# Order of side work beside the tensor engine in a hybrid decoder trunk: sums tied behind newer vector work, loads, squares and scalings spaced differently

## The chip, the cores and the metric

One core of one Trainium2 chip. The metric is the device time of one launch in microseconds (us). The tensor engine is called PE, the vector engine DVE, the scalar engine ACT, GpSimd POOL, and the engine that issues most of the transfers SP. A time of before is the median of several launches; the profile is of one launch of its own.

## The reference

One layer of a decoder trunk over 2048 tokens of width 1024, in float32. All of it is computed from x, a conditioning vector c and the weights:

```python
mod = (c_act @ w_ada[l] + b_ada[l])[:, None, :]
sh1, sc1, g1, sh2, sc2, g2 = jnp.split(mod, 6, axis=-1)
h = rms_norm(x) * (1.0 + sc1) + sh1
x = x + g1 * token_mixer(h, ...)      # retention | HGRN2 | GLA
h = rms_norm(x) * (1.0 + sc2) + sh2
x = x + g2 * conv_ffn(h, ...)         # up, causal conv of width 3, silu gate, down
return rms_norm(x) * final_gain
```

The token mixer projects h once and splits the columns into four retention heads (a fixed decay per head), eight HGRN2 heads and four GLA heads (decays that depend on the data, per key channel). Each group runs a causal linear recurrence over the tokens, gets a norm per head and a swish gate, and one output projection follows.

## The kernel before

The tokens are cut into four blocks b = 0 to 3 of 512. The first part of the program, to about 1140 us, is the mixer: for each block it runs seven units in the order h0, g, h1, h2, h3, r0, r1 (an h unit is two HGRN2 heads, g the GLA heads, an r unit two retention heads), then the output projection in two halves. The rest is the feed-forward part, in two halves of 1024 tokens, with products over sums and differences of blocks (so fewer multiplications), for which sums of the weights and of the activations are made beforehand, during the mixer.

Each float32 product is three PE matmuls on values split into a high and a low part (`split3`, L290 to L292); the high part is a cast on ACT (L278, L342), the low part a subtraction on DVE.

A unit projects (names ps...), then runs its recurrence as a chain of steps (`gated`, `retention`). For an h unit these are: the diagonal dt, masked into `near` on DVE (L722); seven levels lv..._1 to lv..._64, each a PE matmul (L737), after which DVE scales q (L743) and k (L745) for the next level and masks the scores (L749; for wide levels ACT copies, L756, L760); the transposed keys kT (L770, copied by ACT at L773); the update u of the state; `carry`, four steps on DVE (L681) and copies of the state into a wide tile W on ACT (L683, and L674 for the first chunk); the output o (L149), a norm of it (`post`: L630 on ACT, L632, L633, `newton` at L180 to L185, L636, and the gate at L637 on DVE), and its transpose oT (L643). Names carry the unit, the block and the step: `lvh2_2_16` is level 16 of unit h2 in block 2. The gate itself is made in `tok_evac`: ACT copies the values (L613) and takes a sigmoid (L614), DVE multiplies (L615).

What sets the order: PE's instructions stand as the program writes them, and the program is written by a `Clock` that keeps a time of its own in us and calls a step when its due time has come (`clock.at(us, fn)`), a next step of a chain after a gap, or riders at the next level (`ride(fn, soon, late)`). The other engines' instructions, SP's transfers among them, are ordered by the framework's scheduler, by priority. Each engine then takes its instructions strictly in that order. For some side work the program ties the order: `marked(op)` remembers an instruction, and `pinned(fn)` issues what fn emits only after the remembered one. Before, the low-part subtractions (L282, L348, L450) and the k scaling of a level (L745) were marked.

The side work that matters here:

- `ada_next`: a row of the conditioning matrix w_ada is loaded (L264) and, pinned, reduced on DVE (L222).
- `weight_sums` and `early_sums`: two loads (L992, L993), four DVE additions of 128x512 in two steps (L998, L999 and L1002, L1003), two stores (L1005, L1006). `in_turn` runs the steps, pinned, LAND and LAND + 2 us after the loads were called; a second job of a unit comes LAND + 5 after the first.
- `norm1_stat(b + 1)`: the statistics of the next block's first norm. Eight rows x of 128x512 are loaded (L574) STAT_GAP = 2.4 us apart, each squared on ACT (L385, L388) and added on DVE (L389, tile san1); PE sums over partitions (ssn1).
- `out_finish(b)`: the second norm of a block. Its eight scalings t2 (L1077 on DVE, L1078 on ACT, a store at L1079) come NORM_GAP apart. The residual x1 is made at L1058.

Row tiles x, t2 and others share a ring of six buffers (`tmp`); a load into it waits, in SP's queue, until the buffer is free.

Of the kernel before, what the change touches and what calls it, by code (L numbers as in the profile page):

```python
# [14 lines left out]
ALU = mybir.AluOpType  # L15
PSUM = bass.MemoryType.PSUM

P = 128
# [30 lines left out]
M512, M256, MF, ML, MT, MO, MS = 0.227, 0.12, 0.224, 0.5, 0.44, 1.7, 0.85  # L49
LEVEL_GAP = (3.2, 4.2)  # L50
POST_GAP = 14.0
LAND = 6.0
FIRST_GAP = 1.8, 0.8
RIDE = (1.8, 6.0), (3.4, 7.6)
STAT_GAP, NORM_GAP = 2.4, 1.6


class Clock:
# [64 lines left out]
def trunk(ctx, tc, xT, vecs, cvec, cst, rope, msk, wada, win, walow, wgla, wout, wup, wdown, out):  # L123
# [13 lines left out]
    clock = Clock()  # L137
# [8 lines left out]
    def tiled(out, lhs, rhs, start=True, stop=True):  # L146

        for g in range(0, P, 32):
            T.matmul(out[g:g + 32], lhs[:, g:g + 32], rhs(g) if callable(rhs) else rhs, start=start, stop=stop)  # L149
# [12 lines left out]
    def small(name, n=8):  # L162
        return pc.tile([P, n], F32, tag="sm", name=name, bufs=8)

    V, S, G, T = nc.vector, nc.scalar, nc.gpsimd, nc.tensor
# [28 lines left out]
    r = small("lbr", 4)  # L194
# [40 lines left out]
    SH1, SC1, G1, SH2, SC2, G2 = (mod[:, i * 8:i * 8 + 8] for i in range(6))  # L235
# [13 lines left out]
    def marked(op):  # L249

        mark[:] = [op.ins]
# [109 lines left out]
    def rstd(acc, name, bc, then, bank=None, gap=4.5):  # L361

        bank = bank or late_ps

        def first():
            p = bank("ss" + name)
            for c in range(NCH):
                tiled(p[:, c:c + 1], acc[:, c * P:(c + 1) * P], ones)
            x, r = small("ms" + name, NCH), small("rs" + name, NCH)
            with tc.high_priority(offset=CHAIN):  # L370
                V.tensor_scalar(x[:], p[:, 0:NCH], 1.0 / D, EPS, op0=ALU.mult, op1=ALU.add)
                newton(x, r, NCH)
            clock.at(gap, lambda: second(r))

        def second(r):
            p = bank("bc" + name)
            for c in range(NCH):
                T.matmul(p[:, c * P:(c + 1) * P], r[:, c:c + 1].to_broadcast([P, P]), ident, start=True, stop=True)
            S.copy(bc, p[:])
            then()  # L380
        return first

    def sumsq(acc, x, k, name, sl=slice(0, TB), first=None, room=None):
        if k == 0 if first is None else first:
            S.activation(acc[:, sl], x[:, sl], AF.Square)  # L385
        else:
            sq = (room or late)(f"sq{name}{k}")
            S.activation(sq[:, sl], x[:, sl], AF.Square)  # L388
            V.tensor_tensor(acc[:, sl], acc[:, sl], sq[:, sl], op=ALU.add)  # L389
# [15 lines left out]
    bc1 = {}  # L405
    done = set()
# [162 lines left out]
    def norm1_stat(b):  # L569
        acc = new_acc(f"n1_{b}")  # L570

        def part(k):
            x = tmp(f"x{b}_{k}")
            nc.sync.dma_start(x[:], xT[b, :, k, :])  # L574
            sumsq(acc, x, k, f"n1_{b}_")
        for k in range(KD):
            clock.at(STAT_GAP * k, lambda k=k: part(k))
        bc1[b] = new_bc1(b)
        clock.ride(rstd(acc, f"n1_{b}", bc1[b][:], lambda: done.add(("n1", b)), gap=14.0), 24.0, 28.0)

    def norm1_h(b):
        clock.until(lambda: ("n1", b) in done)
# [25 lines left out]
    def tok_evac(vsg, pss):  # L608
        v, sg = vsg
        for j, ps in enumerate(pss):  # L610
            p3 = ps[:].rearrange("p (c n) -> p c n", n=256)
            c2 = slice(2 * j, 2 * j + 2)
            S.copy(v[:, c2, :], p3[:, :, 0:P])  # L613
            S.activation(sg[:, c2, :], p3[:, :, P:256], AF.Sigmoid)  # L614
            V.tensor_tensor(sg[:, c2, :], sg[:, c2, :], p3[:, :, P:256], op=ALU.mult)  # L615

    def tok_evac4(vsg, pss, at):

        v, sg = vsg
        for c, ps in enumerate(pss):  # L620
            gate = ps[:, at + P:at + 256]
            S.copy(v[:, c, :], ps[:, at:at + P])
            S.activation(sg[:, c, :], gate, AF.Sigmoid)
            V.tensor_tensor(sg[:, c, :], sg[:, c, :], gate, op=ALU.mult)

    def post(o, sg, name):

        o8 = o[:].rearrange("p c (h e) -> p (c h) e", e=64)
        sq = late("osq" + name)
        S.activation(sq[:], o[:].rearrange("p c e -> p (c e)"), AF.Square)  # L630
        ms = small("oms" + name)
        V.tensor_reduce(ms[:], sq[:].rearrange("p (a e) -> p a e", e=64), axis=mybir.AxisListType.X, op=ALU.add)  # L632
        V.tensor_scalar(ms[:], ms[:], 1.0 / 64, EPS, op0=ALU.mult, op1=ALU.add)  # L633
        rs = small("ors" + name)
        newton(ms, rs, 8)
        V.tensor_tensor(o8, o8, rs[:].unsqueeze(2).to_broadcast([P, 8, 64]), op=ALU.mult)  # L636
        V.tensor_tensor(o[:], o[:], sg[:], op=ALU.mult)  # L637

    def transposed(b, pos, o, name):

# [250 lines left out]
    def unit_r(b, r, pos):  # L891
        nm = f"r{b}_{r}"
        if r == 0:
            rots[b] = pu.tile([P, NCH, 2, 32], F32, tag="rope", name="rope" + nm, bufs=1)
            nc.sync.dma_start(rots[b][:], rope[b])
        cos, sin = (rots[b][:, :, i, :] for i in range(2))
        kk = pu.tile([P, NCH, P], F32, tag="kk", name="kk" + nm)
        kc = pu.tile([P, TB], F32, tag="k", name="kc" + nm, bufs=3)
        q = p1.tile([P, 2, TB], F32, tag="qbd", name="q" + nm, bufs=3)
        vsg = tok_tiles(nm)  # L900
        pss = tf512("qkvg" + nm, 22 + 4 * r)
        a, bb = ([tmp(f"{n}{i}{nm}") for i in range(2)] for n in ("ra", "rb"))
        for c, ps in enumerate(pss):
            S.copy(a[0][:, c * P:(c + 1) * P], ps[:, 0:P])
            S.copy(a[1][:, c * P:(c + 1) * P], ps[:, P:256])
        tok_evac4(vsg, pss, 256)
        s4 = sin.unsqueeze(2).to_broadcast([P, NCH, 2, 32])
        for x, y in zip(a, bb):
            x8 = x[:].rearrange("p (c g n) -> p c g n", c=NCH, n=32)
            x4 = x[:].rearrange("p (c g t n) -> p c g t n", c=NCH, t=2, n=32)  # L910
            y4 = y[:].rearrange("p (c g t n) -> p c g t n", c=NCH, t=2, n=32)
            V.tensor_tensor(y4[:, :, :, 0, :], x4[:, :, :, 1, :], s4, op=ALU.mult)
            V.tensor_tensor(y4[:, :, :, 1, :], x4[:, :, :, 0, :], s4, op=ALU.mult)
            V.tensor_tensor(x8, x8, cos.unsqueeze(2).to_broadcast([P, NCH, 4, 32]), op=ALU.mult)
            V.tensor_tensor(x4[:, :, :, 0, :], x4[:, :, :, 0, :], y4[:, :, :, 0, :], op=ALU.subtract)
            V.tensor_tensor(x4[:, :, :, 1, :], x4[:, :, :, 1, :], y4[:, :, :, 1, :], op=ALU.add)
        kd = c_all[:, C_KD + 2 * r:C_KD + 2 * r + 2]
        V.tensor_tensor(kk[:].rearrange("p c (h n) -> p c h n", n=64),
                        a[1][:].rearrange("p (c h n) -> p c h n", c=NCH, n=64),
                        kd.unsqueeze(1).unsqueeze(3).to_broadcast([P, NCH, 2, 64]), op=ALU.mult)  # L920
        clock.chain(retention(nm, b, r, pos, a[0], kk, kc, q, vsg), 14.5 if b < 2 else 11.0)

    def retention(nm, b, r, pos, a, kk, kc, q, vsg):
        v, sg = vsg
# [50 lines left out]
    x1 = [None] * KD  # L975
# [35 lines left out]
    def in_turn(*steps):  # L1011
# [6 lines left out]
        for i, _ in enumerate(steps):  # L1018
            clock.at(LAND + 2.0 * i, go)

    def all_done():
        while waiting:
            waiting.pop(0)()
# [21 lines left out]
    def out_half(b, half, acc=None, after_pieces=None, begun=(), own=None):  # L1045
        all_done()
        for i in range(4):
            wp, pss = begun[i] if i < len(begun) else (out_piece(b, half, i), None)
            if i == 3 and after_pieces:
                after_pieces()  # L1050
            for m in (2 * i, 2 * i + 1):
                if half == 0:
                    x1[m] = x_tile(f"x1_{b}_{m}", m)
                    nc.sync.dma_start(x1[m], xT[b, :, m, :])
                ps = pss[m % 2] if pss else acc_ps(f"y{b}_{half}_{m}")
                out_part(b, half, wp, ps, m, range(3, 4) if pss else range(4))
                with tc.high_priority(offset=HOT):
                    V.scalar_tensor_tensor(x1[m], ps[:], G1[:, m:m + 1], x1[m], op0=ALU.mult, op1=ALU.add)  # L1058
                if half == 1:
                    with tc.high_priority(offset=HOT):  # L1060
                        sumsq(acc, x1[m], m, f"n2_{b}_", room=own)
        held[0] -= 4
# [143 lines left out]
    for b in range(NB):  # L1206
        pos = 0
# [4 lines left out]
        for i, (kind, u) in enumerate(ORDER):  # L1212
# [4 lines left out]
            if b and i:  # L1217
# [5 lines left out]
                for n, fn in enumerate(job):  # L1223
                    clock.at((30.0 if i == 1 else 14.0 if (b, i) == (1, 4) else 0.1) + (LAND + 5.0) * n, fn)
            mk[kind](b, u, pos)
# [17 lines left out]
    with tc.high_priority(offset=300):  # L1243
        A = {}
        for i in range(2):
            r = tmp(f"r0{i}_0_0")
# [382 lines left out]
    for k in range(4):  # L1629
        x = t2k(f"hr0_3_{k}")  # L1630
# [117 lines left out]
```

## Time and profile before

| | us |
|---|---|
| median of 3 runs | 2422.54 |
| lowest, highest run | 2421.09, 2425.87 |
| profiled execution | 2418.1 |
| its span | 2416.3 |
| PE busy in the span | 2382.3 |
| DVE busy | 1811.7 |
| ACT busy | 1229.3 |
| PE idle, all of the span | 34.0 |

The profiled execution takes 1.8 us more than its span. PE's idle time is the span less its busy time; 16.0 us of it lie before 120 us, 5.9 between 120 and 1080, and 12.2 after. In a list of waits each row names who waited, for whom (the instruction that ended last by the profile, which need not be the one whose data was needed), how long in total, how often, and the longest. In a timeline each row has the start, the duration, the engine, the line, the operation, the tiles, and in brackets the idle time of the engine before it with its releaser; several instructions that follow each other are one row with a count.

### The profile page before, as it was taken

What the parts mean: (1) busy time and instruction counts of PE and PEld (TensorE: products, weight loads), DVE (VectorE), ACT (ScalarE), POOL (GpSimd) and SP (SyncE); (2) the same over time, 40 slices, a digit from 0 to 9 for tenths busy, and PEclk for the clock granted to TensorE, in tenths of its full rate; (3) what the DMA queues carried; (4) which work ended last, traced back from release to release, by engine and by line L of the source; (5) the groups of instructions that cost most, each with busy time, mean ns of one, the idle gap of its engine ahead of it and who ended that gap; (6) DMA issues with size and microseconds to landing.
All of it is one profiled execution on the core that took longest, in us unless ns stands there. A gap on an engine that the chain in (4) does not pass through costs nothing.

```text
span 2416.3 us, 51796 instructions
## 1 busy us (share of the span) xinstructions
PE 2382.3 (99%) x20523; PEld 1962.8 (81%) x20523; DVE 1811.7 (75%) x3391; ACT 1229.3 (51%) x2191; POOL 154.2 (6%) x275
## 2 busy tenths in 40 slices
PE   7999999999999999999999999999999999999998
PEld 5788878878788878888788888888878888888887
DVE  7687766877577746767988888966878787778666
ACT  4565445644565446535645554554545454555442
POOL 1000000000000000001000000000010110000000
PEclk9999999999999999999999999999999999999999
DMA  7665676896788758778554444686765444447663
GB/s 273 228 214 186 226 271 224 293 329 237 258 311 290 259 187 284 267 260 295 178 170 155 148 155 144 229 281 218 226 204 173 144 149 139 153 151 271 210 196 118
DMA packets 228883, 525.78 MB, mean 218 GB/s; under 512 B 25848, under 2 KB 28832, under 8 KB 228640
## 3 DMA queue, kind: packets, MB, share of 16 engines
q1 hardware_dynamic: 225440, 511.98, 63.1%
q0 software_dynamic: 3200, 10.49, 1.2%
q8 instruction: 161, 2.64, 0.4%
q14 instruction: 82, 0.67, 0.1%
HBM read 392.87 MB, written 129.50 MB: 216 GB/s over the span
## 4 chain that ended last, share of the span: by engine, by line
PE 84%; DVE 6%; DMA 5%; issue 3%; ACT 1%; SPq 0%; POOL 0%; DVEq 0%; ACTq 0%; POOLq 0%
PE X L290 6%; PE X L291 6%; PE X L292 6%; PE Z L291 3%; PE Z L292 3%; PE Z L290 3%; PE dX L290 3%; PE dX L292 3%; PE dX L291 3%; PE psqkvgr L290 3%; PE psqkvgr L291 2%; PE psqkvgr L292 2%; PE psvgh L290 2%; PE y L290 2%; PE y L291 2%
## 5 line engine op out<-in xcount | busy, mean ns | idle before, releaser
L290 PE MATMUL X<-B,A 128*128 128x512 f32 x572 | 223.1, 390 | 0.5 <-ACT u L1424 0.3
L291 PE MATMUL X<-B,A 128*128 128x512 f32 x572 | 222.8, 389 | 0.3 <-DVE B L1121 0.2
L292 PE MATMUL X<-B,A 128*128 128x512 f32 x572 | 222.6, 389 | 0.0
L1121 DVE TENSOR_TENSOR dA<-rd,dA 128x512 fp32r<-128x512 f32 x154 | 106.1, 690 | 89.8 <-ACT dA L1120 89.6
L1120 ACT CAST dA<-rd 128x512 fp32r<-128x512 f32 x154 | 95.6, 621 | 143.7 <-PE dX L292 58.0
L290 PE MATMUL dX<-dB,dA 128*128 128x512 f32 x396 | 154.1, 389 | 1.3 <-DVE y L1606 1.3
L292 PE MATMUL dX<-dB,dA 128*128 128x512 f32 x396 | 154.0, 389 | 0.0
L291 PE MATMUL dX<-dB,dA 128*128 128x512 f32 x396 | 154.0, 389 | 0.0
L1121 DVE TENSOR_TENSOR A<-s,A 128x512 fp32r<-128x512 f32 x176 | 120.6, 686 | 39.5 <-ACT A L1120 39.4
L290 PE MATMUL psvgh<-hvgh,ha 128*128 128x256 f32 x480 | 140.3, 292 | 0.0
L1120 ACT CAST A<-s 128x512 fp32r<-128x512 f32 x176 | 108.5, 617 | 56.9 <-PE Z L292 41.9
L291 PE MATMUL psvgh<-lvgh,ha 128*128 128x256 f32 x480 | 135.6, 283 | 0.0
L292 PE MATMUL psvgh<-hvgh,ha 128*128 128x256 f32 x480 | 135.6, 282 | 0.0
L290 PEld LDWEIGHTS X<-B,A 128*128 128x128 f32 x572 | 107.3, 188 | 24.0 <-ACT u L1424 1.1
L291 PEld LDWEIGHTS X<-B,A 128*128 128x128 f32 x572 | 107.4, 188 | 23.0 <-DVE B L1121 1.0
L292 PEld LDWEIGHTS X<-B,A 128*128 128x128 f32 x572 | 107.4, 188 | 22.3
L291 PE MATMUL Z<-B,A 128*128 128x512 f32 x308 | 120.5, 391 | 1.4 <-DVE B L1121 1.2
L290 PE MATMUL Z<-B,A 128*128 128x512 f32 x308 | 120.3, 391 | 0.1
L292 PE MATMUL Z<-B,A 128*128 128x512 f32 x308 | 119.9, 389 | 0.0
L1120 ACT CAST A<-r 128x512 fp32r<-128x512 f32 x132 | 82.3, 623 | 63.8 <-PE Z L292 58.5
L1121 DVE TENSOR_TENSOR A<-r,A 128x512 fp32r<-128x512 f32 x132 | 90.6, 687 | 31.8 <-ACT A L1120 31.6
L1121 DVE TENSOR_TENSOR dB<-rb,dB 128x512 fp32r<-128x512 f32 x154 | 105.6, 687 | 9.9 <-ACT dB L1120 9.5
(480 smaller groups left out, 6714.3 us busy)
## 6 DMA issues: line engine op xcount, KB each, us to landing
gs<-yv SPq DMA_DIRECT2D x154, 256.0 KB, 3.0
rb<-gs SPq DMA_DIRECT2D x154, 256.0 KB, 4.2
r<-wup SPq DMA_DIRECT2D x143, 256.0 KB, 3.5
s<-sumsu SPq DMA_DIRECT2D x132, 256.0 KB, 3.0
wada<-wada SPq DMA_DIRECT2D x48, 512.0 KB, 4.9
rd<-sumsd SPq DMA_DIRECT2D x88, 256.0 KB, 3.9
rd<-wdown SPq DMA_DIRECT2D x66, 256.0 KB, 3.8
x<-xT SPq DMA_DIRECT2D x64, 256.0 KB, 5.9
```

The costliest lines, as they stand in the source:

```text
L290: T.matmul(ps, lhs[0], rhs[0], start=first, stop=False, skip_group_check=more)
L291: T.matmul(ps, lhs[0], rhs[1], start=False, stop=False, skip_group_check=more)
L292: T.matmul(ps, lhs[1], rhs[0], start=False, stop=last, skip_group_check=more)
L1120: S.copy(hi, src)
L1121: V.tensor_tensor(lo, src, hi, op=ALU.subtract)
```

## The change

Five edits; no instruction is added or taken away on any engine, only places in the queues change.

```diff
-LAND = 6.0
+LAND = 7.5
-STAT_GAP, NORM_GAP = 2.4, 1.6
+STAT_GAP, STAT_LAND, NORM_GAP = 2.4, 3.0, 2.0
...
         def part(k):
             x = tmp(f"x{b}_{k}")
             nc.sync.dma_start(x[:], xT[b, :, k, :])
-            sumsq(acc, x, k, f"n1_{b}_")
+            clock.at(STAT_LAND, lambda: sumsq(acc, x, k, f"n1_{b}_"))
...
-        clock.ride(rstd(acc, ...), 24.0, 28.0)
+        clock.ride(rstd(acc, ...), 26.0, 30.0)
...
-            V.tensor_tensor(sg[:, c2, :], sg[:, c2, :], p3[:, :, P:256], op=ALU.mult)
+            marked(V.tensor_tensor(sg[:, c2, :], sg[:, c2, :], p3[:, :, P:256], op=ALU.mult))
...
-            V.tensor_tensor(sg[:, c, :], sg[:, c, :], gate, op=ALU.mult)
+            marked(V.tensor_tensor(sg[:, c, :], sg[:, c, :], gate, op=ALU.mult))
...
-        V.tensor_tensor(o[:], o[:], sg[:], op=ALU.mult)
+        marked(V.tensor_tensor(o[:], o[:], sg[:], op=ALU.mult))
...
-        clock.chain(retention(nm, b, r, pos, a[0], kk, kc, q, vsg), 14.5 if b < 2 else 11.0)
+        clock.chain(retention(nm, b, r, pos, a[0], kk, kc, q, vsg), 14.5 if b < 3 else 11.0)
...
-                    V.scalar_tensor_tensor(x1[m], ps[:], G1[:, m:m + 1], x1[m], op0=ALU.mult, op1=ALU.add)
+                    marked(V.scalar_tensor_tensor(x1[m], ps[:], G1[:, m:m + 1], x1[m], op0=ALU.mult, op1=ALU.add))
```

The gate products (L615, L624), the last product of `post` (L637) and the residual (L1058) are now marked, so pinned work stands behind them. Sums fall due 1.5 us later after their loads, a second job 12.5 instead of 11 us after the first. A row's square is called 3.0 us after its load. t2 scalings are 2.0 instead of 1.6 apart. The retention of block 2 starts 3.5 us later by the program's clock, as that of blocks 0 and 1 does already. On PE only that last edit is seen: the matmuls of r2_0 and r2_1 stand some 3.5 us later among the others; elsewhere PE's list is the same.

DVE, unit h2 of block 1, the carry of the state (L681, tiles Sc and S2) before the output oh1_2; wsd1 is a weight sum. Before:

```order
L749 COPY_PREDICATED nearh1_3_0_6758<-m_all_87,lvh1_3_2_6876 128x64x2
L681 SCALAR_TENSOR_TENSOR Sc_6918<-S2_107,eh1_2_5628,uh1_2_6901 128x64
L998 TENSOR_TENSOR wsd1_2_6813<-wsd1_1_6812 128x512
L681 SCALAR_TENSOR_TENSOR Sc_6918<-Sc_6918,eh1_2_5628,uh1_2_6901 128x64
L999 TENSOR_TENSOR wsd1_2_6813<-wsd1_2_6813,wsd1_0_6811 128x512
L681 SCALAR_TENSOR_TENSOR Sc_6918<-Sc_6918,eh1_2_5628,uh1_2_6901 128x64
L1002 TENSOR_TENSOR wsd1_0_6811<-wsd1_0_6811,wsd1_1_6812 128x512
L681 SCALAR_TENSOR_TENSOR S2_107<-Sc_6918,eh1_2_5628,uh1_2_6901 128x64
```

And now, at the same place:

```order
L749 COPY_PREDICATED nearh1_3_0_6758<-m_all_87,lvh1_3_2_6881 128x64x2
L681 SCALAR_TENSOR_TENSOR Sc_6918<-S2_107,eh1_2_5628,uh1_2_6901 128x64
L681 SCALAR_TENSOR_TENSOR Sc_6918<-Sc_6918,eh1_2_5628,uh1_2_6901 128x64 x2
L681 SCALAR_TENSOR_TENSOR S2_107<-Sc_6918,eh1_2_5628,uh1_2_6901 128x64
L998 TENSOR_TENSOR wsd1_2_6813<-wsd1_1_6812 128x512
```

The four carry steps stand together, and the sum begins behind them.

ACT, unit h1 of block 1, before the output oh1_1_0, which reads W0; x2_4 is a row of block 2's first norm. Before:

```order
L817 ACTIVATE kh1_3_6134<-snh1_3_6342,oml_89 128x512
L1078 ACTIVATE t2_0_6_6358<-t2_0_6_6358,mod_102 128x512
L683 COPY W0_112<-Sc_6332 64x3x64 x2
L1078 ACTIVATE t2_0_7_6374<-t2_0_7_6374,mod_102 128x512
L674 COPY W0_112<-S5_110 64x64 x2
L388 ACTIVATE sqn1_2_4_6364<-x2_4_6362 128x512
```

And now:

```order
L817 ACTIVATE kh1_3_6134<-snh1_3_6334,oml_89 128x512
L278 CAST hvgh1_3_1_6625<-rvgh1_3_1_6627 128x1024
L388 ACTIVATE sqn1_2_4_6398<-x2_4_6349 128x512
L683 COPY W0_112<-Sc_6324 64x3x64 x2
L1078 ACTIVATE t2_0_5_6355<-t2_0_5_6355,mod_102 128x512
L1078 ACTIVATE t2_0_6_6372<-t2_0_6_6372,mod_102 128x512
```

A cast and the square of x2_4, which both need a load, now stand ahead of the copies into W0, and the scaled rows t2 behind them.

DVE, unit h2 of block 2, between the levels 8 and 32 (san1_3 is the sum of squares for block 3, omsh2_1_0 and orsh2_1_0 the norm of unit h1's output). Before:

```order
L697 TENSOR_TENSOR eh2_3_10092<-eh2_3_10092 128x4
L389 TENSOR_TENSOR san1_3_10088<-san1_3_10088,sqn1_3_5_10319 128x512
L389 TENSOR_TENSOR san1_3_10088<-san1_3_10088,sqn1_3_6_10394 128x512
L632 TENSOR_REDUCE omsh2_1_0_10400<-osqh2_1_0_10398 128x8
L743 TENSOR_TENSOR qbh2_2_9821<-qbh2_2_9821,eh2_2_9567 128x64x8
L633 TENSOR_SCALAR omsh2_1_0_10400<-omsh2_1_0_10400 128x8
L745 TENSOR_TENSOR kh2_2_9565<-kh2_2_9565,eh2_2_9567 128x32x8
```

And now, from the second half of the norm on:

```order
L745 TENSOR_TENSOR kh2_2_9565<-kh2_2_9565,eh2_2_9567 128x32x8
...
L389 TENSOR_TENSOR san1_3_10088<-san1_3_10088,sqn1_3_6_10465 128x512
L636 TENSOR_TENSOR oh2_1_0_10339<-oh2_1_0_10339,orsh2_1_0_10397 128x512
L826 TENSOR_TENSOR sqh2_3_10425<-sqh2_3_10425,fh2_3_10091 128x512
L637 TENSOR_TENSOR oh2_1_0_10339<-oh2_1_0_10339,sgh2_1_9316 128x512
L743 TENSOR_TENSOR qbh2_2_9821<-qbh2_2_9821,eh2_2_9567 128x32x16
L745 TENSOR_TENSOR kh2_2_9565<-kh2_2_9565,eh2_2_9567 128x16x16
L749 COPY_PREDICATED nearh2_2_0_10125<-m_all_87,lvh2_2_16_10523 128x8x16
L389 TENSOR_TENSOR san1_3_10088<-san1_3_10088,sqn1_3_7_10500 128x512
```

The addition of x3_6 has moved from ahead of L743 and L745 of level 8 to behind them, and the end of the norm now stands ahead of those of level 16.

More of the change, by code (lines that the diff above doesn't have):

```diff
@@ L578, in norm1_stat @@
         bc1[b] = new_bc1(b)
-        clock.ride(rstd(acc, f"n1_{b}", bc1[b][:], lambda: done.add(("n1", b)), gap=14.0), 24.0, 28.0)
+        clock.ride(rstd(acc, f"n1_{b}", bc1[b][:], lambda: done.add(("n1", b)), gap=14.0), 26.0, 30.0)
     def norm1_h(b):
```

## The prediction

> **What bounds the kernel now.** I read the page first: the engines' busy time, then the windows of the tensor engine (PE), to see how much idle time the touched stretch holds at all.
>
> ```profile
> PE 2382.3 (99%) x20523; PEld 1962.8 (81%) x20523; DVE 1811.7 (75%) x3391; ACT 1229.3 (51%) x2191; POOL 154.2 (6%) x275
> 120.00:1080.00 960.00, 954.11 (x13240) 1.00 0.74 256
> 360.00:480.00 120.00, 118.59 (x1944) 1.00 0.75 257
> 720.00:840.00 120.00, 117.79 (x1659) 1.00 0.80 277
> ```
>
> PE is the bound, 99% busy at a granted clock of 1.00. The order lists first differ near 150 us and agree again near 1130 us; the counts of instructions don't change. In 120 to 1080 us PE is idle for 960.00 - 954.11 = 5.9 us. No edit takes PE work away, so **5.9 us (0.24%) is the most this change can take out of that execution**, while what it can add has no such lid. Next the waits of PE, to see whose fault that idle time is.
>
> ```profile
> PE lvh L737 <- DVE orsh L180: 1.5, 1, 1.5
> PE kTh L770 <- DVE nearh L722: 1.0, 1, 1.0
> PE psqkvgr L291 <- issue: 1.0, 1, 1.0
> PE oh L149 <- DVE S L681: 0.4, 1, 0.4
> PE lvh L737 <- DVE nw L184: 0.4, 1, 0.4
> PE kTh L770 <- DVE kh L745: 0.3, 1, 0.3
> PE oh L149 <- ACT W L683: 0.3, 1, 0.3
> PE oTh L643 <- DVE oh L637: 0.3, 1, 0.3
> ```
>
> Columns: waiter, releaser, total us, times, longest. These eight make 5.2 of the 5.9 us. "issue" is nobody's data. The names of the vector engine (DVE) behind the arrow are only the instructions that happened to end last; what held them stands in the timeline.
>
> **Place 1, 480 us: a weight sum in front of a carry.**
>
> ```profile
> 478.46 0.69 DVE L998 TENSOR_TENSOR wsd<-wsd 128x512 f32<-128x512 f32 x1 [1.75 <-DMA wsd<-wdown]
> 479.86 0.28 DVE L681 SCALAR_TENSOR_TENSOR Sc<-Sc,eh,uh 128x64 f32<-128x64 f32 x1
> 481.07 0.38 PE L149 MATMUL oh<-W,qbh 128*32 128x128 f32 x5 [0.44 <-DVE S L681]
> wsd<-wdown SPq DMA_DIRECT2D x22, 512.0 KB, 5.6
> wsu<-wup SPq DMA_DIRECT2D x22, 512.0 KB, 5.9
> ```
>
> DVE stood 1.75 us for a load that had not landed, three of the four carry steps L681 queued behind it, ACT's copies L683 behind those, PE's oh1_2_0 behind these. In the new order all four carry steps stand ahead of L998 (marks), and the sum comes due 7.5 instead of 6.0 us after its load, against median landings of 5.6 and 5.9. The 0.44 goes: **-0.4**. The DVE work is only moved; what follows the sum then is lvh1_3_4's masks, which in this execution cause no wait.
>
> **Place 2, 439 us: gate products, and what the earlier row does in ACT's queue.**
>
> ```profile
> 436.92 0.35 ACT L613 COPY vh<-psvgh 128x256 f32<-128x256 f32 x1
> 437.58 0.42 DVE L615 TENSOR_TENSOR sgh<-sgh,psvgh 128x256 f32<-128x256 f32 x1 [0.65 <-ACT sgh L614]
> 438.86 0.43 DVE L722 COPY_PREDICATED nearh<-m_all,dth 128x256 f32<-128x256 uint32 x1
> 439.35 0.66 PE L770 MATMUL kTh<-c_all,kh 128*128 128x128 f32 x4 [0.99 <-DVE nearh L722]
> 447.48 0.70 ACT L683 COPY W<-Sc 64x192 f32<-64x192 f32 x2
> 447.92 0.45 PE L149 MATMUL oh<-W,qbh 128*32 128x128 f32 x8
> ```
>
> DVE waited 0.65 us for ACT's sigmoid, and ACT came late because scaled rows t2 (L1078) and a square stood ahead of L613. With t2 rows 2.0 apart and the square 3.0 behind its load, ACT has two of these fewer ahead of it; by my count of the new order the chain L613, L614, L615, L743, L745, L722 ends about 1.0 us earlier, and the 0.99 goes: **-1.0**.
>
> The same shift plants a new wait. In the new ACT queue the cast L278 and the square of x2_4 stand ahead of the two L683 copies; before, both came elsewhere. PE would now want W at 447.92 - 0.99 = 446.93. How long such rows take to land:
>
> ```profile
> x<-xT SPq DMA_DIRECT2D x64, 256.0 KB, 5.9
> 437.41 0.43 SPq L574 DMA_DIRECT2D x<-xT  x1
> 441.34 0.63 ACT L388 ACTIVATE sqn<-x 128x512 f32<-128x512 f32 x1 [0.24 <-DMA x<-xT]
> 420.09 0.43 SPq L574 DMA_DIRECT2D x<-xT  x1
> 428.46 0.63 ACT L385 ACTIVATE san<-x 128x512 f32<-128x512 f32 x1 [0.47 <-DMA x<-xT]
> ```
>
> From issue to the square that waited for it: 441.34 - 437.41 = 3.9 us for x2_3, 428.46 - 420.09 = 8.4 for x2_0; the median is 5.9. In the new SP queue x2_4 stands behind rqkvgr1_0_0, and I place its issue at 442.1 (an estimate). Landing after 3.9, 5.9 or 8.4 us, plus a square (0.63) and the copies (0.70), W is ready at 447.3, 449.3 or 451.8: a wait of 0.4, 2.4 or 4.9. I take a landing of 4.8, between the two nearest rows (3.9, and the median): **+1.3**, ends 0.4 and 4.9.
>
> [...]
>
> **Place 3, 458 us.**
>
> ```profile
> 457.59 0.42 DVE L745 TENSOR_TENSOR kh<-kh,eh 128x256 f32<-128x256 f32 x1
> 458.16 0.46 PE L737 MATMUL lvh<-qbh,kh 128*32 128x32 f32 x32 [0.37 <-DVE nw L184]
> ```
>
> lvh1_2_16 waited 0.4 for L745, behind L389 and L632 which ACT delivered late. The new order has the norm's chain and L821 ahead, ACT's osq square no longer sits behind three squares, and L745 should end about a us earlier: **-0.4**.
>
> **Place 4, 735 us: the largest wait.**
>
> ```profile
> 731.30 0.63 ACT L388 ACTIVATE sqn<-x 128x512 f32<-128x512 f32 x1 [2.81 <-DMA x<-xT]
> 731.97 0.69 DVE L389 TENSOR_TENSOR san<-san,sqn 128x512 f32<-128x512 f32 x1 [1.72 <-ACT sqn L388]
> 733.44 0.69 DVE L389 TENSOR_TENSOR san<-san,sqn 128x512 f32<-128x512 f32 x1 [0.78 <-ACT sqn L388]
> 734.65 0.68 DVE L743 TENSOR_TENSOR qbh<-qbh,eh 128x512 f32<-128x512 f32 x1
> 735.32 0.42 DVE L745 TENSOR_TENSOR kh<-kh,eh 128x256 f32<-128x256 f32 x1
> 735.88 0.46 PE L737 MATMUL lvh<-qbh,kh 128*32 128x32 f32 x32 [1.49 <-DVE orsh L180]
> 740.05 0.43 PE L737 MATMUL lvh<-qbh,kh 128*32 128x64 f32 x16
> 740.30 0.27 PE L149 MATMUL ssn<-c_all,san 128*32 128x1 f32 x14
> 724.01 2.36 SPq L574 DMA_DIRECT2D x<-xT  x3
> ```
>
> The squares asked for rows that had not landed; ACT stood 2.81 us, DVE 1.72 + 0.78, and L743/L745 for lvh2_2_16 stood behind. In the new order x3_2 to x3_5 are issued ahead of weight loads and sum stores in SP's queue, and x3_6's addition stands behind L745. DVE's 2.5 us of standing cover the 1.49 with 1.0 to spare: **-1.5**. Paid back next: lvh2_2_32 and the sum ssn1_3 would be wanted at 738.56 and 738.81. Ahead of them on DVE now stand the addition of x3_6, then L636, L826, L637 and L743/L745. x3_6 goes out behind the store L1006 of sumsu11, which waits for L1003, now behind lvh2_2_4's masks: about 727.9 (an estimate; x3_5 to x3_7 went out from 724.01 on in the last row above). With 5.9 us it lands at 733.8; square 0.63, addition 0.69, four steps of 0.69 and one of 0.42: 738.3, and with L749 and x3_7's addition (0.29 + 0.69) ssn1_3 is ready at 739.3, a wait of 0.5. With 8.4 us it is 3.0. I take **+0.7**, since each step also costs a hand-over. Then oTh2_1_0's 0.3 goes, its L637 standing four places earlier: **-0.3**.
>
> **The rest at nothing.** Of the eight waits, kTh L770 0.3 (same DVE order there), oh W 0.3 (178 us, ACT's own copies) and "issue" stay. The retention of b = 2 starts 3.5 us later in PE's own list: PE fills in with projection matmuls that stood there anyway, and the consumer of its last tile, y2_1, stands some 85 rows behind it; no wait between 840 and 1080 us gives it anything to win. t2's scalings (eight, L1077) only spread over 14.0 instead of 11.2 us; their stores are read in b = 3 at the earliest. If the retention's chain loses its cover, the nearest row is a hand-over like the 0.4 of oh.
>
> **Sum.** -0.4 - 1.0 + 1.3 - 0.4 - 1.5 + 0.7 - 0.3 = -1.6 us. The profiled execution took 2418.1 (span 2416.3 and 1.8 around it) and would take 2416.5. The median of the runs shown, 2422.54, lies 4.4 above it, so other executions wait more than this one shows, most likely for landings; I carry the difference over: 2422.54 - 1.6 = **2420.9**. A measurement of this kernel can tell about 0.2%, 4.8 us, from no change.
>
> **Rivals.** *Everything goes, nothing comes back.* The waits that the change reaches make 0.4 + 1.0 + 0.4 + 1.5 + 0.3 = 3.6 here. If the 4.4 us by which other runs are longer are landing waits of the same two kinds (sums and squares asked for too early), and half of them go too, it is -5.8: 2416.7. For it: median landings (5.6 to 5.9) sit right at the old 6.0. Against: PE shows only 3.6, and ACT's new order puts squares ahead of copies. Chance 0.24, all of it faster.
>
> *Slower: squares block ACT.* The rows are loaded earlier but their squares also stand earlier in ACT's queue, ahead of the W copies and the casts. It decides once rows land later than some 6 us. At 8.4: +4.9 instead of +1.3 at 447 us, +3.0 at 739 us, and x2_3's square ahead of kTh1_1's copy holds uh1_1 as well; if half of the 3.6 is lost in that queue, it is 4.9 + 3.0 - 1.8 = +6.1: 2428.6. For it: x2_0 did take 8.4. Against: the loads were moved ahead of other transfers. Chance 0.19, slower.
>
> *Nothing moves.* PE's list is nearly the same, and each wait freed is met by the next: 2422.5. Chance 0.09.
>
> **How the numbers follow.** The forecast has 0.48, with its own range of 2418.9 (gains of 3.6 and no new wait) to 2424.3 (new waits of 2.4 and 3.0), all within 0.2%. Same is 0.48 + 0.09 = 0.57, faster 0.24, slower 0.19. The range for 8 in 10 runs from 2416.0, just under the first rival, to 2428.0, just under the second.
>
> **What would show it.** Right: L998 of wsd1 behind all L681 with no DVE wait before the carry; no wait at lvh1_2_16, lvh2_2_16, oh1_2_0; the standing of ACT at L388 and of DVE at L389 near 731 us gone; small new waits at oh1_1_0 (releaser ACT L683) and ssn1_3 or lvh2_2_32. Wrong: PE's idle time in 120 to 1080 us above 5.9, or new waits after 780 us at the moved retention.

## The result and the profile after

| | median, us | lowest to highest | profiled execution's span |
|---|---|---|---|
| before | 2422.5 | 2419.9 to 2427.1 (9 runs) | 2416.3 |
| after | 2429.8 | 2425.8 to 2433.0 (9 runs) | 2424.2 |

The changed kernel is slower: ratio 1.0025, 95% interval 1.0016 to 1.0035, some 6 us; the medians lie 7.3 us apart and the two spans 7.9. The forecast was 2420.9 in a range of 2416.0 to 2428.0.

The profile after, first the busy line of the page and the windows of the tensor engine (columns: stretch, its length, PE busy, granted clock, DMA share, GB/s).

```profile
PE 2385.8 (98%) x20523; PEld 1964.8 (81%) x20523; DVE 1816.5 (75%) x3391; ACT 1232.6 (51%) x2191; POOL 153.8 (6%) x275
120.00:1080.00 960.00, 949.48 (x13170) 1.00 0.75 256
360.00:480.00 120.00, 116.99 (x1932) 1.00 0.76 260
600.00:720.00 120.00, 117.61 (x1643) 1.00 0.84 281
720.00:840.00 120.00, 117.29 (x1660) 0.99 0.81 283
```

PE's idle time between 120 and 1080 us has gone from 5.9 to 10.5 us, and over the whole span PE is also busy 3.5 us longer for the same matmuls (the half clock shown below makes 1.7 of that by my estimate; the rest isn't explained). The waits of PE in that stretch say where; its six largest new rows are these.

```profile
PE oh L149 <- issue: 2.7, 1, 2.7
PE kTh L770 <- DVE kh L745: 1.9, 1, 1.9
PE lvg L737 <- ACT atg L756: 1.4, 3, 0.7
PE oTg L643 <- DVE oTg L648: 1.2, 1, 1.2
PE lvh L737 <- issue: 0.9, 1, 0.9
PE oh L149 <- ACT W L683: 0.8, 1, 0.8
```

The waits that the change was to remove (lvh1_2_16, kTh1_1, oh1_2_0, lvh2_2_16, oTh2_1_0) are gone. These six came in their place, and only the last of them had a term in the forecast. Two kinds carry most of it.

**A reduction that waits for its row.** The timeline near kTh2_0 (607 us before, 610 now):

```profile
600.37 1.28 DVE L222 CUSTOM_DVE_ANT_0 wada<-wada,c_act,vec 128x1024 f32<-128x1024 f32 x1
601.69 0.33 SPq L264 DMA_DIRECT2D wada<-wada  x1
606.89 1.28 DVE L222 CUSTOM_DVE_ANT_0 wada<-wada,c_act,vec 128x1024 f32<-128x1024 f32 x1 [2.07 <-DMA wada<-wada]
609.96 0.41 DVE L745 TENSOR_TENSOR kh<-kh,eh 128x256 f32<-128x256 f32 x1
610.43 0.66 PE L770 MATMUL kTh<-c_all,kh 128*128 128x128 f32 x4 [1.93 <-DVE kh L745]
```

Rows of w_ada have one buffer. The load (L264) can go only when the reduction before it (L222) is over, at 601.69; the next reduction stands 2.07 us for it, and L745, for which PE waits, stands behind in the vector engine's queue. The vector engine's waits in the same stretch, of before and then of after:

```profile
DVE wada L222 <- DMA wada<-wada: 17.0, 10, 4.2
```
```profile
DVE wada L222 <- DMA wada<-wada: 24.4, 17, 3.2
```

Ten such stands have become seventeen.

**A stop for which no data is missing.** In the moved retention, the timeline of PE and three windows:

```profile
797.94 1.16 PE L950 MATMUL scr<-qr,kcr 64*32 64x128 f32 x64
799.03 0.42 PE L149 MATMUL oh<-W,qbh 128*32 128x128 f32 x8
...
800.60 0.29 PE L149 MATMUL oh<-vh,ath 128*32 128x64 f32 x7
803.60 0.33 PE L149 MATMUL oh<-vh,ath 128*32 128x64 f32 x9 [2.71 <-issue]
804.46 0.63 PE L292 MATMUL psqkvgr<-hqkvgr,ha 128*128 128x512 f32 x1
804.00:806.00 2.00, 2.00 (x6) 0.59 1.04 396
806.00:808.00 2.00, 2.00 (x6) 0.56 1.08 415
804.36:807.77 3.41, 3.41 (x9) 0.50 1.07 407
```

and of before, at the same matmuls:

```profile
793.03 1.16 PE L950 MATMUL scr<-qr,kcr 64*32 64x128 f32 x64
794.11 0.50 PE L290 MATMUL psqkvgr<-hqkvgr,ha 128*128 128x512 f32 x1
...
798.64 0.29 PE L149 MATMUL oh<-vh,ath 128*32 128x64 f32 x7
799.34 0.35 PE L149 MATMUL oh<-vh,ath 128*32 128x64 f32 x9 [0.41 <-issue]
```

PE stops in the middle of oh2_3_0, 2.71 us instead of 0.41, and then, from 804.36 on, runs at a granted clock of 0.50 for 3.4 us; half of that, 1.7 us, is my estimate of what it costs further. Before, twelve projection matmuls stood between scr2_0 and oh2_3_0; now the two follow each other directly.

### The profile page after: what moved, and what is told of

Read it like the earlier page. It is cut to its first block, busy times and chain, and to the rows that moved or that the text cites. A ratio compares the mean times of both kernels' runs of the same rounds, so it can differ in the third digit from the quotient of the medians.

```text
span 2424.2 us, 51792 instructions
## 1 busy us (share of the span) xinstructions
PE 2385.8 (98%) x20523; PEld 1964.8 (81%) x20523; DVE 1816.5 (75%) x3391; ACT 1232.6 (51%) x2191; POOL 153.8 (6%) x275
## 4 chain that ended last, share of the span: by engine, by line
PE 83%; DVE 6%; DMA 6%; issue 2%; ACT 2%; SPq 0%; DVEq 0%; POOL 0%; ACTq 0%; POOLq 0%
PE X L290 6%; PE X L292 6%; PE X L291 6%; PE Z L291 3%; PE Z L292 3%; PE Z L290 3%; PE dX L290 3%; PE dX L291 3%; PE dX L292 3%; PE psqkvgr L290 3%; PE psqkvgr L291 2%; PE psqkvgr L292 2%; PE y L290 2%; PE psvgh L290 2%; PE y L291 2%
```

## The experiments

Two theories came out of these readings: A, that PE ran out of instructions in the moved retention, and C, that reductions tied later keep the one row buffer; their rivals (B, D to G) stand with the runs. In the table L222 is the vector engine's total stand for rows of w_ada between 120 and 1080 us; "stop" is PE's wait near 800 us in oh2_3_0 with releaser issue, each in the one profiled execution.

| kernel | ratio to before, 95% interval | L222: us, times | stop, us |
|---|---|---|---|
| before | | 17.0, 10 | 0.41 |
| after | 1.0025, 1.0016 to 1.0035 | 24.4, 17 | 2.71 |
| marks_alone | 1.0030, 1.0018 to 1.0042 | 25.6, 16 | 1.51 |
| marks_rows_only | 1.0020, 1.0010 to 1.0031 | 29.4, 15 | 0.39 |
| rows_old_marks | 1.0007, 0.9999 to 1.0016 | 14.5, 10 | 2.13 |
| two_rows | 1.0007, 0.9998 to 1.0016 | 1.5, 2 | 2.33 |
| marks_two_rows | 0.9994, 0.9985 to 1.0003 | 2.0, 2 | 1.58 |
| two_rows_before | 0.9995, 0.9986 to 1.0003 | 2.5, 4 | 1.50 |
| ret_alone | 1.0011, 1.0002 to 1.0020 | 18.3, 10 | 2.67 |
| ret_undone | 1.0021, 1.0009 to 1.0033 | 26.9, 17 | 0.50 |
| ret_16_0 | 1.0002, 0.9993 to 1.0011 | 18.3, 10 | none |
| ret_12_5 | 1.0003, 0.9994 to 1.0012 | 18.8, 10 | none |
| stat_alone | 1.0002, 0.9993 to 1.0011 | 18.3, 11 | 1.31 |
| land_alone | 1.0004, 0.9995 to 1.0013 | 18.9, 10 | none |
| norm_alone | 1.0003, 0.9994 to 1.0012 | 17.0, 10 | 0.94 |
| land_norm | 1.0017, 1.0008 to 1.0026 | 17.7, 9 | none |
| best2 | 0.9996, 0.9987 to 1.0005 | 1.8, 2 | none |
| best3 | 0.9990, 0.9981 to 0.9999 | 1.3, 1 | 0.38 |
| best3_again | 1.0000, 0.9991 to 1.0009 | 1.9, 2 | 0.31 |
| best4 | 0.9994, 0.9985 to 1.0003 | 1.3, 1 | 0.25 |

### The marks

```diff
 marks_alone, from the kernel before: only the four new marked(...) at L615, L624, L637, L1058
```

> The kernel before with the four new marks alone (gate products L615 and L624, L637, L1058). Theory C: reductions of the rows of w_ada (L222) are tied later, the single buffer of those rows comes free later, the next row's load with it, and DVE then stands 1.5 to 2 us for it with level scalings L743 and L745 behind; that gives PE waits of about 2 us at kTh2_0 (607 us) and 1 us at lvg1_64 (401 us), against gains of 0.4 at oh1_2_0 and 1.0 at kTh1_1: +1 to +3 us in sum. By the prediction: -0.4 to -2, since the carry and L745 stand ahead of the sums.

1.0030: +7.1 us by itself, as much as the whole change and more than expected; the prediction's gain is refuted. At kTh2_0 PE waits 0.71 here, less than the 2 us expected. At lvg1_64 the wait is there as expected:

```profile
394.91 1.28 DVE L222 CUSTOM_DVE_ANT_0 wada<-wada,c_act,vec 128x1024 f32<-128x1024 f32 x1 [1.42 <-DMA wada<-wada]
397.56 0.69 DVE L826 TENSOR_TENSOR sqh<-sqh,fh 128x512 f32<-128x512 f32 x1
398.29 1.25 ACT L828 COPY qbh<-sqh 64x512 f32<-64x512 f32 x2 [5.96 <-DVE sqh L826]
406.04 0.67 PE L737 MATMUL lvg<-qbg,kg 64*32 64x128 f32 x30 [0.68 <-ACT atg L756]
```

The reduction's stand pushes L826 on the vector engine, for which ACT's queue stands 5.96 us (2.63 before), and the copies L756 behind it come late for lvg1_64. This wait of 0.9 to 1.0 us in all (two stops) stands in the profiles of the four kernels that tie the reductions behind the new marks and have one buffer, and in no other. Not every place tells the causes apart so well: at oh0_1_0 (179 us) PE waits 1.26 behind a stand of L222 here, but 1.49 in marks_two_rows and 1.99 in best2 (both below), where L222 doesn't stand there.

To tell the reductions from the sums, which are tied by the same marks, two lists of marks were kept:

```diff
-    def pinned(fn):
+    def pinned(fn, behind=mark):
-        with tc.issue_after(mark[0]):
+        with tc.issue_after(behind[0]):
 rows_old_marks, from the changed kernel: new marks enter only mark2
-                pinned(waiting.pop(0))
+                pinned(waiting.pop(0), mark2)
 marks_rows_only, from the kernel before with the new marks in mark2
-            pinned(lambda: ada(*loaded.pop()))
+            pinned(lambda: ada(*loaded.pop()), mark2)
```

> The changed kernel with the reductions of the rows of w_ada (L222) tied behind the old marks only; the sums stay behind the new ones, the other edits are kept. In the vector engine's waits between 120 and 1080 us, L222 stood for its row 17.0 us in 10 cases before, 24.4 in 17 in the changed kernel and 25.6 in 16 with the marks alone. Theory C (a reduction tied later frees the one buffer later, the next row is loaded later, the next reduction stands for it with carries and level scalings behind): L222 waits back at 16 to 19 us in 10 or 11 cases, and 3.5 to 6.5 us of the 7.3 go (ratio to before 1.0003 to 1.0016). Theory E (it is the sums behind the newer marks that crowd the vector engine): L222 aside, the time stays at 1.002 to 1.0035.

> The kernel before with the new marks for the reductions L222 alone; the sums stay tied to the old marks. Theory C: nearly all of the 7.1 us that the four marks cost by themselves, +4 to +7.5 us (ratio 1.0017 to 1.0031), L222 waits 24 to 27 us in 16 or 17 cases. Theory E: within 1.5 us of before.

Both times are as theory C has it: 1.0007 (the stands at 14.5 us in 10 cases, even under what was expected) and 1.0020 (29.4 in 15, more than the 24 to 27 expected). Theory E falls with them. Its direct opposite is to take the wait itself away and leave every tie where the change put it (the second pair of lines makes room for the second buffer):

```diff
 two_rows from the changed kernel, two_rows_before and marks_two_rows from the kernel before
-            raw = p1.tile([P, D], F32, tag="wada", name=f"wada{m}", bufs=1)
+            raw = p1.tile([P, D], F32, tag="wada", name=f"wada{m}", bufs=2)
-    mod = pc.tile([P, 48], F32, tag="mod", name="mod")
+    mod = vec[:, V_BADA:V_BADA + 48]
```

> The changed kernel with a second buffer for the rows of w_ada (mod moved into columns of another tile to make room), so that a row's load no longer waits for the reduction just before. Theory C: L222 waits under 6 us in all, the time 4 to 7 us under the changed kernel (ratio to before 0.9995 to 1.0013; the moved retention's 2 to 3 us stay). Theory E: 1.002 to 1.0035, as the changed kernel.

> The kernel before with the second buffer for the rows of w_ada. Theory C: L222's 17.0 us of standing fall under 6; the tensor engine waited little behind it there, so 0 to -3 us (ratio 0.9988 to 1.0000). Rival: rows of 512 KB issued earlier crowd the transfers of weights and of x, and the time rises by 1 to 3 us.

> The kernel before with the four new marks and the second buffer for the rows of w_ada, nothing else. Theory C: the marks' whole cost of 7.1 us was the rows' loads, so it stands where the second buffer alone does, 0.9985 to 1.0003, with L222 waits under 6 us. If the marks cost in another way too (sums and squares in new places): 1.0008 or more.

With a second buffer L222 stands 1.5 us in all, and the changed kernel comes down to 1.0007. With the marks alone and the second buffer the 7.1 us are gone altogether (0.9994, no different from the second buffer without the marks, 0.9995). So the marks' cost is the rows' one buffer, and nothing else that these runs can see. The kernel before had 17.0 us of such stands also; taking them away gave it nothing that can be measured (two_rows_before, 0.9995), and the rival's loss from crowded transfers didn't come either.

### The retention of block 2

```diff
 ret_alone, ret_16_0, ret_12_5 from the kernel before: 14.5, 16.0, 12.5 for b == 2
-  ... 14.5 if b < 2 else 11.0)
+  ... 14.5 if b < 3 else 11.0)
 ret_undone from the changed kernel: back to 14.5 if b < 2
```

> The kernel before with one edit alone: the retention of block 2 starts 3.5 us later (14.5 for b < 3). Theory A (PE ran out of instructions): in the changed kernel the 32 matmuls of scr2_0 and the 96 of oh2_3_0 stand directly together, PE stopped there for 2.7 us with the releaser issue, and the granted clock then fell to half for 3.4 us; that comes from the order alone, so this edit by itself gives +3 to +6 us over the kernel before, a wait with the releaser issue of over 2 us near 800 us at oh L149, and a stretch with a granted clock of 0.5 to 0.6 right behind it. Theory B (queues of the vector and scalar engines: squares and late sums): the retention's move is worth -1 to +1 us, and no clock dip is seen.

> The changed kernel with the retention of block 2 back at its old place (14.5 for b < 2), the other four edits kept. Theory A: some 4.5 of the 7.3 us go, so 2.5 to 3 us over the kernel before (ratio 1.001), no clock dip behind 800 us. Theory B: stays 6 to 8 us over the kernel before (ratio 1.0025 to 1.0035).

> The kernel before with the retention of block 2 at 16.0 instead of 11.0. On PE oh2_3_0 then stands directly ahead of scr2_0, so the two runs of small matmuls are still together, in the other order. Theory A (PE stops where such a run meets a late block of its instructions): a wait with releaser issue of over 2 us there, +2 to +4 us. Rival (the cost grows with how late the retention runs, through its chain): no such wait, +3 to +5 us from other waits at or, oTr or kTr.

> The kernel before with the retention of block 2 at 12.5 instead of 11.0: 12 projection matmuls still stand between scr2_0 and oh2_3_0, as before. Theory A: within 1.5 us of before, the wait with releaser issue near 800 us under 1.6 us and no fall of the clock. Rival (the cost grows with the delay): +1 to +1.5 us.

Alone the move costs 1.0011, some 2.7 us, just under what was expected, with the same stop of 2.67 us and a fall of the granted clock behind it (0.99 in the mean of 720 to 840 us). Its interval, 1.0002 to 1.0020, is 0.5 to 4.8 us. Undone from the changed kernel it gives less than expected (1.0021, between what A and B had, with both inside its interval), but undone beside the second buffer the ratio falls by 0.0011 again (two_rows 1.0007, best2 0.9996, a difference that is itself within the error). So the stop is shown, and what it costs is known only roughly. All four kernels with 14.5 stop for 2.1 to 2.7 us, all others for 0 to 1.6.

What lands just before PE goes on there can be read from the transfers. The page after has, among its queues,

```profile
q8 instruction: 161, 2.64, 0.4%
```

161 blocks of 16 KB, for 20523 matmuls and 20523 weight loads. No row names the engine that reads them; from the start of one to the start of the next PE began 127 matmuls in the mean, 18 to 269 in the profile of before and 19 to 269 in that of after. So I took a block for 256 of PE's instructions, or 128 matmuls (an estimate). In the six kernels of the list below that stop, the stop stands before the same matmul, the 10517th or its neighbour, and ends 1.2 to 1.5 us after a block has landed. From the records of that queue and of PE:

```
kernel          the 128 matmuls   they    next block fetched   PE goes on at,
                before began at   took    from, in             after the fetch's end
before          793.50            5.4     796.96, 0.96         799.34, 1.42
after           798.23            2.7     801.21, 0.94         803.60, 1.45
ret_alone       799.82            2.7     802.94, 0.93         805.16, 1.29
rows_old_marks  794.20            2.7     796.68, 0.93         798.99, 1.38
two_rows        791.88            2.7     794.25, 1.37         796.86, 1.24
marks_alone     799.65            5.4     804.25, 1.01         806.59, 1.33
ret_16_0        797.92            2.5     797.65, 0.91         no stop
```

At 14.5 these 128 matmuls are all small ones, and PE is through with them in 2.7 us; in the old order twelve projection matmuls are among them and it takes 5.4. In all these but ret_16_0 the next block's fetch begins 2.4 to 4.6 us after the first of them, in both orders, and in the new one PE was through with them before that block had landed, and stood (land_alone and land_norm, which have the old order, show no stop). ret_12_5 is as theory A has it: 1.0003 and no stop here. ret_16_0 tells that neither the delay nor small matmuls side by side are enough: its 128 matmuls are as short (2.5 us), and theory A expected a stop of over 2 us and +2 to +4 us there; it has no stop and 1.0002, and its fetch went out 0.3 us before they began. The rival (a cost that grows with the delay) fell with it. That PE had run out of instructions is read from this order of events alone. What lets a fetch go out is not settled; in the profiles of before and after these fetches fall in stretches of 2 us in which the DMA engines are 92 to 101% busy, and thinning them was not tried.

### Squares and spacings

```diff
 stat_alone: clock.at(STAT_LAND, lambda: sumsq(...)) with 3.0, and the end at 26.0, 30.0
 land_norm:  LAND = 7.5 and NORM_GAP = 2.0;  land_alone, norm_alone: one of the two
```

> The kernel before with the first norm's squares 3.0 us behind their loads alone (and its end 2 us later). By the prediction: the stand of ACT at L388 near 731 us and the wait of 1.5 at lvh2_2_16 go, -1 to -2 us. By theory D (squares now stand ahead of the copies into W and of L647 on ACT, and hold them where a row lands late): new waits of some 1 us each at oTg1_1 and oh1_1_0 near 441 to 450 us, in sum 0 to +2 us.

> The kernel before with the two spacings alone: sums 7.5 instead of 6.0 behind their loads (a second job 1.5 later), t2 scalings 2.0 instead of 1.6 apart. By the prediction a wait less at oh1_2_0 and kTh1_1: -1.4 us. By the sum of the parts (marks 7.1, retention 2.7, squares 0.5, together 10.3, against 7.3 for all five) these two would have to give -3 us, unless the parts overlap; then 0.

> The kernel before with the sums 7.5 instead of 6.0 behind their loads, alone. Theory F (without the new marks the later steps of a sum come to stand in a norm's chain: in the kernel with both spacings all four steps of wsd6 stood between the steps of the norm of oh2_1_0, and oTh2_1_0 waited 1.7 us): +2 to +4 us, a wait over 1 us at oTh2_1_0 near 745 us. Theory G (the wider scalings cost it): -1 to +1 us. The prediction had -0.4.

> The kernel before with the t2 scalings 2.0 instead of 1.6 apart, alone. Theory G (a further scaling L1077 of 0.75 us then stands ahead of L637 of oh3_0_0, and oTh3_0_0 waits 1.3 us near 920 us; the like at other blocks): +1.5 to +4 us. Theory F: -1 to +1 us. The prediction had -1.0.

The squares alone change nothing (1.0002): neither the gain that the prediction had from them nor theory D's loss. In the profile the 1.49 at lvh2_2_16 does go, but ssn1_3 waits 1.21 in its place, and theory D's waits at oTg1_1 and oh1_1_0 are 0.51 and 0.32. The two spacings together cost 1.0017 where a gain or nothing was expected, but each by itself 1.0004 and 1.0003, so neither F nor G has its loss. F's wait is there: in land_alone the four steps of a sum stand in a norm's chain and oTh2_1_0 waits 1.9 (1.7 in land_norm). G's is in land_norm alone, where a further scaling stands ahead of L637 of oh3_0_0; norm_alone shows no wait there. First land_alone, then land_norm:

```profile
PE oTh L643 <- DVE rsn L180: 1.9, 1, 1.9
```
```profile
920.01 0.74 DVE L1077 SCALAR_TENSOR_TENSOR t<-x,mod,bc 128x512 f32<-128x512 f32 x1
921.47 0.68 DVE L637 TENSOR_TENSOR oh<-oh,sgh 128x512 f32<-128x512 f32 x1
922.30 0.63 PE L643 MATMUL oTh<-c_all,oh 128*128 128x128 f32 x4 [1.34 <-DVE eg L697]
```

But 1.0 and 0.7 us don't make 4.1 (each with an error of some 2 us, so chance isn't ruled out), and the parts alone (7.1, 2.7, 4.1, 0.5) sum to 14 where the whole costs 6 to 7. That the parts overlap is plain, in what way the spacings do is open.

### Versions with both causes taken away

```diff
 best2: the changed kernel, two row buffers, retention back
 best4: best2 with NORM_GAP = 1.6;  best3, best3_again: best4 with LAND = 6.0
```

> The changed kernel with the second buffer for the rows of w_ada and the retention of block 2 back at its old place: both causes found so far taken away, the marks, the sums at 7.5, the squares behind their rows and the wider scalings kept. If the costs add up, the kernel with the second buffer (ratio 1.0007) less the retention's 0.0011: 0.9996, -2 to +1 us; L222 waits under 6 us, no wait with releaser issue above 1.6 us near 800 us.

> As the run with marks, squares and second row buffer, with the sums at 7.5 also. If the new marks take the later sums' cost away (the sum then stands behind L637 of the norm): the same as without, within 1 us. If the sums cost beside the marks too: +2 to +4 us over it.

> The kernel before with three things: the four new marks, the squares 3.0 us behind their loads and the second buffer for the rows of w_ada (sums at 6.0 and scalings 1.6 apart as before, retention as before). If the marks pay once the rows' cost is gone: 0.9980 to 0.9995 (-1 to -5 us), better than with the spacings (0.9996). If not, 0.9995 to 1.0005.

> The kernel with marks, squares 3.0 us behind their loads and the second row buffer once more. If it is faster: ratio 0.998 to 0.9997 again. If the first was luck: 0.9997 to 1.0006.

best2 met its expectation, 0.9996: with the second buffer and the old place of the retention the change costs nothing. So rows (1.0025 to 1.0007) and retention (1.0007 to 0.9996) together carry the whole loss. The first step is clear of the error, the second is not by itself, so how they share the loss is known only roughly. best3 was 0.9990 once and 1.0000 when repeated: all of them beat the changed kernel, none is shown to beat the one before. best4 is the same as best3 within the error, so beside the marks the later sums cost nothing that can be measured.

## Why the prediction was wrong

**Place by place the waits went as forecast, in one place not by the edit it named.** oh1_2_0, kTh1_1, lvh1_2_16, lvh2_2_16 and oTh2_1_0 wait no longer. The new wait for W0, forecast at 1.3, is there with 0.84, by the row and the releaser that were named:

```profile
447.21 1.06 ACT L278 CAST hvgh<-rvgh 128x1024 fp32r<-128x1024 f32 x1 [0.90 <-DMA rvgh<-win]
449.37 0.63 ACT L388 ACTIVATE sqn<-x 128x512 f32<-128x512 f32 x1 [1.09 <-DMA x<-xT]
449.91 0.70 ACT L683 COPY W<-Sc 64x192 f32<-64x192 f32 x2
450.66 0.42 PE L149 MATMUL oh<-W,qbh 128*32 128x128 f32 x8 [0.84 <-ACT W L683]
```

x2_4 went out at 443.62 and its square began at 449.37: 5.8 us against the 4.8 taken. The 0.7 at lvh2_2_32 and ssn1_3 didn't come. At 480 us the carry does stand ahead of the sum, but 7.5 us didn't cover the landing, and the vector engine stood longer than before, only where nobody waits for it:

```profile
479.39 0.28 DVE L681 SCALAR_TENSOR_TENSOR S<-Sc,eh,uh 128x64 f32<-128x64 f32 x1
483.13 0.69 DVE L998 TENSOR_TENSOR wsd<-wsd 128x512 f32<-128x512 f32 x1 [3.46 <-DMA wsd<-wdown]
```

The prediction gave the marks the credit for that order. With the marks alone (marks_alone) L998 still stands between the first and the second L681, and oh1_2_0 waits 1.01, more than before; with the sums at 7.5 alone (land_alone) the four steps stand together and oh1_2_0 doesn't wait. So it was the later sums that took this wait away.

By these terms alone it would have been -0.4 - 1.0 + 0.8 - 0.4 - 1.5 - 0.3 = -2.8 in that profile.

**The step that failed is "the rest at nothing".** It left out one user of the marks. `pinned` also ties `ada_next`'s reductions, and I followed only the sums. A reduction that stands later frees the one row buffer later, and the next load goes out later; the price is not the reduction's 1.28 us but a stand for a landing (2.07 us ahead of kTh2_0). Where the prediction said of kTh L770 "same DVE order there" and kept 0.3, the order was the same and the wait 1.93, because the row landed later. Measured, taking the wait for the rows away is worth some 4.4 us (1.0025 to 1.0007), against a term of 0.

**The retention was mis-sized.** It was taken at 0, with a hand-over of 0.4 as the nearest row if the cover went. It costs some 2.7 (ret_alone). The argument was about data: no wait between 840 and 1080 us, projection matmuls as cover, a consumer 85 rows on. No data wait came at the moved retention, but the cover went: the twelve projection matmuls no longer stand between scr2_0 and oh2_3_0, and PE stopped for 2.71 us with no data missing, until 1.45 us after a block of q8 had landed. The profile of before had a row for that, "issue" (1.0 at psqkvgr), and the prediction set it aside as nobody's data and as staying. Its list left out a second such row of that stretch, which stands at the very matmul where the changed kernel stops for 2.71:

```profile
PE oh L149 <- issue: 0.4, 1, 0.4
```

**One new wait was put in the wrong case.** At oTg1_1 (443 us) the vector engine stands 1.89 us for the square of x2_3 with L648 behind it, and PE waits 1.20 for L648. The prediction had that square only in the slower rival. The marks play a part there too: with them alone PE waits 1.10 at this place.

**The rivals.** "Squares block ACT" gave 2428.6, close to the 2429.8 measured, but by luck: the squares alone cost nothing (stat_alone). "Everything goes" rested on the 4.4 us by which the median lay above the profile; that the difference is landing waits that the change could take is not borne out. Carrying the difference over, as the forecast did, held: the median of after lies 3.8 us above its profiled execution.

**One profile is a coarse ruler.** ret_alone, ret_12_5 and ret_16_0 have the order of the kernel before up to some 780 us. The wait of lvh1_2_16 (PE lvh L737 <- DVE nw L184), 0.4 in the profile of before, was 2.2, 1.5 and 0.9 in these, and the one of lvh2_2_16, 1.5 in the profile of before, was 0.8, 2.4 and 0.7. Terms of 0.3 to 0.4 out of one execution were finer than the thing repeats.

## What to carry to other kernels

When a tie or a priority is changed, list everything that goes through it, and of each such instruction ask which buffer it frees and which load waits for that buffer: with a single buffer a small move was paid here with a landing, and a second buffer took that cost away. When an order is changed on the engine that bounds, look at "issue" in its waits also: the new order of the retention was free of data waits here, and yet PE stopped in it for 2.71 us, until 1.45 us after a block of q8 had landed. A sum of terms under 2 us from one execution needs a second execution before it is believed.

## What the hardware showed that was not expected

The queue q8 of instructions brought 161 blocks of 16 KB in the profiles of before and of after, one for every 127 of PE's matmuls in the mean, and in the kernels of the list above that stop, PE went on 1.2 to 1.5 us after a block's 0.9 to 1.4 us fetch had ended, at the same matmul or its neighbour.

A stop of PE was paid twice at times here. In the changed kernel the stop of 2.71 us was followed by 3.413 us at a granted clock of 0.50, in which matmuls of 128x512 began 0.43 us apart, where they began 0.23 apart just before scr2_0: up to 1.7 us more, by my estimate. The clock fell behind four stops of other kernels too: ret_alone 2.67 (0.99 in the mean of 720 to 840 us) and 2.25 (matmuls of 128x256 began 0.21 us apart for some 3 us, before and after that 0.12), rows_old_marks 2.13 (0.93 in the mean of 788 to 812 us) and ret_undone 1.75 (0.99 in the mean of 480 to 600 us). It did not behind 2.42 in ret_12_5 (0.12 apart from the second matmul on, as before the stop), 2.33 in two_rows (1.00 in 788 to 812 us) and 1.93 at kTh2_0 in the profile after (1.00 in 600 to 720 us). So the length of a stop alone doesn't tell these cases apart: the clock fell behind one of 1.75 us and not behind one of 2.42.
